# An attention and RWKV layer kernel: attention's loads one by one and a group ahead, groups in a new order, one bias load a head, and 8.0 instead of 1.5 between the inverse and its products

## The chip, the cores and the metric

The kernel runs on one core of one Trainium2 chip. The time is the device time of one launch in microseconds, the median of several runs. The core has five engines that the text names: TensorE (PE) for matmuls, VectorE (DVE), ScalarE (ACT), GpSimd (POOL), and SyncE (SP), which here only issues DMAs.

## The reference

Two trunk layers run over 128 context tokens and 512 latent tokens (a grid of 8 rows of 64), 1024 wide, in fp32. Each layer is

```python
proj = (x * (1 + scale1) + shift1) @ w_in
mix  = concat([o_rwkv, o_na, o_g], -1) @ w_out
x    = layer_norm(alpha * x + gate1 * mix)
gate, up = split((x * (1 + scale2) + shift2) @ w_ffn_in)
x    = layer_norm(alpha * x + gate2 * ((silu(gate) * up) @ w_ffn_out))
```

Three mixers read `proj`. RWKV (4 heads of 64) is a scan over the tokens in both directions:

```python
sk = einsum('bhvk,bhk->bhv', s, kk_t)
s  = s * w_t - sk * (a_t * kk_t) + v_t * k_t      # o_t = s @ r_t
```

Neighbourhood attention (na, 4 heads) lets a latent token see a window of 16 columns in all 8 rows, with a bias by relative position, and the context cache; columns outside are masked:

```python
s_nb = where(in_win, q @ kb * scale + rpb[:, dr, dc], NEG_INF)
p    = softmax(concat([s_nb, q @ k_ctx * scale]))
```

Grouped-query attention (gqa, 8 query heads on 2 key heads, RMS-normed and rotary) has each latent token see all latent tokens and 256 cached ones. Context tokens attend to context alone. Besides the two outputs the RWKV end states and the keys and values of the context are returned.

## The kernel before, in words

Everything stays transposed, features on partitions and tokens along the free axis. A product of fp32 weights is three matmuls on a high and a low part (`xh,whi`, `xl,whi`, `xh,wlo`), 320 tokens wide. Per layer the stages are the input projection (`proj_all`), `mixing` (attention), `mixed` (the output projection by w_out), and the tail with the feed-forward part.

**RWKV** is cut into chunks of 64 tokens, as 8 jobs per layer (two pairs of heads, two halves, two directions) in two slots of four jobs that run side by side. `rwkv_slot` takes each job through features, products, `inverse` and `states`. `inverse` (L757 to L800) inverts small triangular blocks on VectorE, copies the result into the tile `TB`, writes it and `XB` to DRAM by two DMAs from ScalarE's queue (`td<-TB` L793, `xd<-XB` L794) and reads them back in matrix form by four DMAs from GpSimd's queue (`T<-td` L797, `X<-xd` L799). Then it yields 1.5 (L800). `states` begins with a product that doesn't need them (`RV,N`); its second is `T,A` on PE, which needs `T`. From there on each product reads what the one before left: `N,X` and `X,N`, `T,A`, `X,N`, `AL,X`, `RV,ST` and `ST,RV`, `ST,A`, `S,A`, `RHO,S`; then the group norm of a finished half (`f,bmean`, `bmean,gnsq`, `ident,gnr`). I call this row of products the chain of a job.

**Attention** consists of units: six context pairs (`ctx_pair`), two na groups of four units (`na_pair`), four gqa groups of four units (`gqa_pair`), in this order. A unit makes scores of two heads (`ks,qs`), softmax on VectorE and ScalarE, transposes of the probabilities (`ident,prob`) and the products with the values (`pT,vw`, `pT,nvc`, `pT,gv`, `pT,gvc`); a group ends with `ident,sms`. The data come back from DRAM by SyncE's queue: queries `qs` (`stacked`, 256 KB, 4 buffers), keys `ks` (`doubled`, 2 x 384 KB, 3 buffers), the na values `vw` (`na_values`, 8 DMAs of 64 KB, 1 buffer) and the na bias (`na_bias`, 4 DMAs a head of 128x8x32 words, 2 buffers), to which GpSimd adds the column mask (L949). All loads of a group are written at once, where the group begins; those of the first group are written before the context pairs (`load_attn`).

**What sets the order.** Tasks are generators. `yield x` means: come back when the planner's clock `te.now` has gone on by x microseconds; this clock is the modelled time of the PE work that was emitted. `tick` steps all tasks that are due; `weave` steps the one that is due first, and sets the clock forward if none is. In `mixing` two attention tasks and RWKV's two slots run through `weave` until attention is at its end; `mixed` then begins the output projection and ticks through what RWKV has left. From the text thus written a scheduler sets each engine's order, and on the chip each engine runs its list in that order.

Of the kernel before, what the change touches and what calls it, by code (L numbers as in the profile page):

```python
# [8 lines left out]
F32 = mybir.dt.float32  # L9
F32R = mybir.dt.float32r  # L10
AF = mybir.ActivationFunctionType
ALU = mybir.AluOpType
# [4 lines left out]
P = 128  # L17
# [4 lines left out]
NLAT = 512  # L22
# [9 lines left out]
NA_LO = (0, 8, 24, 32)  # L32
NA_N = 32
# [50 lines left out]
class Build:  # L84
# [547 lines left out]
    def rwkv_job(self, l, ft, hb, d, slot, pool):  # L632
# [121 lines left out]
        def inverse():  # L754

            BT = J.BT
            bt = lambda name, n, tag=None: pool.tile([4 * NC] + n, F32, name=f"{name}{slot}", tag=f"{tag or name}{slot}", bufs=1)  # L757
            XB = bt("XB", [16, 16], "rt3")
            tmp = bt("tmpB", [512], "rt2")
            nc.gpsimd.memset(XB, 0.0)  # L760
            nc.gpsimd.memset(XB.rearrange("p i j -> p (i j)")[:, ::17], 1.0)

            def q8(t, i, j0, j1):

                b = t[:, 0, 0:1]
                return bass.AP(tensor=b.tensor, offset=b.offset + i * 16 + j0, ap=[list(b.ap[0]), [8 * 17, 2], [1, j1 - j0]])

            def q8m(t, i0, i1, j0, j1):

                b = t[:, 0, 0:1]  # L770
                return bass.AP(tensor=b.tensor, offset=b.offset + i0 * 16 + j0, ap=[list(b.ap[0]), [8 * 17, 2], [1, j1 - j0], [16, i1 - i0]])
            for i in range(6, -1, -1):
                m = 7 - i
                if m == 1:
                    nc.vector.tensor_copy(q8(XB, i, i + 1, 8), q8(BT, i, i + 1, 8))
                    continue
                t = tmp[:, :2 * m * m].rearrange("p (q k j) -> p q k j", q=2, k=m)
# [24 lines left out]
        def bmm(lhs, rhs, N, evac, swap=False):  # L802

# [117 lines left out]
    def load_attn(self, l):  # L921
        nc, I, at = self.nc, self.I, self.at
        self.nvc = at.tile([P, 2, 256], F32, name="nvc", bufs=1)
        nc.gpsimd.dma_start(self.nvc, I["c_na_v"][l])
        self.gvc = at.tile([P, 2, P], F32, name="gvc", bufs=1)
        self.units_ = self.units(l)
        first = next(self.units_)
        self.units_ = itertools.chain([first], self.units_)
        nc.gpsimd.dma_start(self.gvc, I["c_g_v"][l])

    def na_values(self, l, ft):

        nc = self.nc
        vw = self.at.tile([P, 4, 2, P], F32, name="vw", bufs=1)
        vr = self.vd.rearrange("(r c) f -> r c f", c=64)[:, :, ft * P:(ft + 1) * P]
        for j in range(4):
            for hf in range(2):
                nc.sync.dma_start(vw[:, j, hf, :], vr[hf * 4:hf * 4 + 4, NA_LO[j]:NA_LO[j] + NA_N, :])  # L938
        return vw

    def na_bias(self, l, hd):

        nc = self.nc
        bias = self.at.tile([P, 4, 8, NA_N], F32, name="bias", bufs=2)
        for j in range(4):
            b = self.rpx[0:1]
            off = hd * 15 * 16 * (RP - 1) + PAD + 15 + NA_LO[j] - 16 * j
            nc.sync.dma_start(bias[:, j], bass.AP(tensor=b.tensor, offset=b.offset + off, ap=[[RP - 1, P], [16 * (RP - 1), 8], [1, NA_N]]))  # L948
            nc.gpsimd.tensor_tensor(bias[:, j], bias[:, j], bc(self.nmask[:, j * NA_N:(j + 1) * NA_N], 1, 8), ALU.add)  # L949
        return bias  # L950

    def stacked(self, dram, h, name, n, bufs):

# [1 line left out]
        self.nc.sync.dma_start(self.r32(t), dram[:, h * CH:(h + 1) * CH, :])  # L955
        return t

    def doubled(self, dram, h):

        t = self.at.tile([P, 2, 768], F32R, name="ks", tag="ks", bufs=3)  # L960
        for u in range(2):
            self.nc.sync.dma_start(self.r32(t[u * CH:(u + 1) * CH]), dram[:, h * CH:(h + 1) * CH, :].rearrange("a p n -> p a n"))
        return t

    def out_parts(self, dram, hi, lo):
        self.nc.sync.dma_start(dram[0], self.r32(hi))
# [131 lines left out]
            yield from unit  # L1098

    def units(self, l):  # L1100
        def load(ft):
            bias = [self.na_bias(l, 2 * ft + h) for h in range(2)]
            vw, ks = self.na_values(l, ft), [self.doubled(self.nkd[ft], h) for h in range(2)]
            return vw, [(self.stacked(self.nqd[ft], h, "qs", NLAT, 4), ks[h], bias[h]) for h in range(2)]
        vw, qk = load(0)
        for kt in range(6):
            yield self.ctx_pair(l, kt)
        for ft in range(2):
            if ft:
                vw, qk = load(ft)  # L1110
            st = {}
            for j in range(4):
                yield self.na_pair(l, ft, j, qk, vw, st)
        for kv in range(2):
            ks = self.doubled(self.gkd, kv)
            for m in range(2):
                qs = [self.stacked(self.gqd[2 * m + u], kv, "qs", NLAT, 4) for u in range(2)]
                st = {}
                for t in range(4):
                    yield self.gqa_pair(l, kv, m, t, qs, ks, st)  # L1120

    def softmax(self, ps, n, negmax, scale, sums=None):

# [70 lines left out]
    def na_pair(self, l, ft, j, qk, vw, st):  # L1194
        nc = self.nc
# [4 lines left out]
        for h in range(2):  # L1200
# [10 lines left out]
            nc.vector.tensor_tensor_reduce(ps[:, 0:nw], ps[:, 0:nw], bias[:, j].rearrange("p r n -> p (r n)"), 1.0, mc, ALU.add, ALU.max, mx)  # L1211
# [400 lines left out]
```

## Time and profile before

| | |
|---|---|
| runs | 2167.08, 2173.63, 2172.19 us; median 2172.19 |
| the profiled execution | 2173.96 us, span 2172.2 us |
| PE busy | 2056.1 us (95%) |
| VectorE, ScalarE, GpSimd busy | 1304.0 us (60%), 909.6 us (42%), 250.5 us (12%) |
| chain that ended last | PE 78%, DMA 9%, DVE 5%, ACT 3%, issue 2% |
| DMA | 226.48 MB in 158276 packets, 88533 of them under 512 B |

The span of layer 0's attention is about 291 to 577 us, of layer 1's 1334 to 1635 us; the long stretches between and behind are the feed-forward parts and the projection. The busy line of the page's second part, 40 slices of 54 us, shows them: attention lies in slices 6 to 11 and 25 to 30, where PE's digits and those of the granted clock go down to 7 and 8. [...]

### The profile page before, as it was taken

What the parts mean: (1) busy time and instruction counts of PE and PEld (TensorE: products, weight loads), DVE (VectorE), ACT (ScalarE), POOL (GpSimd) and SP (SyncE); (2) the same over time, 40 slices, a digit from 0 to 9 for tenths busy, and PEclk for the clock granted to TensorE, in tenths of its full rate; (3) what the DMA queues carried; (4) which work ended last, traced back from release to release, by engine and by line L of the source; (5) the groups of instructions that cost most, each with busy time, mean ns of one, the idle gap of its engine ahead of it and who ended that gap; (6) DMA issues with size and microseconds to landing.
All of it is one profiled execution on the core that took longest, in us unless ns stands there. A gap on an engine that the chain in (4) does not pass through costs nothing.

```text
span 2172.2 us, 41222 instructions
## 1 busy us (share of the span) xinstructions
PE 2056.1 (95%) x16737; PEld 1863.3 (86%) x16737; DVE 1304.0 (60%) x2874; ACT 909.6 (42%) x1823; POOL 250.5 (12%) x435
## 2 busy tenths in 40 slices
PE   6989989799999999999999999879999999999997
PEld 4877877577889999999989887657779999999997
DVE  6536677586776666666766567657767533233247
ACT  3434455455563212222466445546555421221234
POOL 0012242121100000000020224311101000000000
PEclk9999998899999999999999999879999999999998
DMA  8555354110414444444431415521114122222223
GB/s 296 147 155 167 108 107 91 41 44 20 153 63 142 150 145 156 146 146 144 142 133 69 134 64 106 99 55 27 32 45 138 61 74 73 72 70 84 77 84 111
DMA packets 158276, 226.48 MB, mean 104 GB/s; under 512 B 88533, under 2 KB 99413, under 8 KB 157957
## 3 DMA queue, kind: packets, MB, share of 16 engines
q1 hardware_dynamic: 118244, 200.82, 29.7%
q0 software_dynamic: 7568, 17.83, 3.0%
q10 hardware_dynamic: 32274, 5.20, 1.4%
q8 instruction: 132, 2.16, 0.4%
q14 instruction: 58, 0.48, 0.1%
HBM read 198.37 MB, written 25.40 MB: 103 GB/s over the span
## 4 chain that ended last, share of the span: by engine, by line
PE 78%; DMA 9%; DVE 5%; ACT 3%; issue 2%; SPq 1%; POOL 0%; ACTq 0%; POOLq 0%; DVEq 0%
PE ps_s L72 44%; PE ps_rw L72 26%; PE ps_pv L72 5%; PE ps_rw L76 4%; DMA td<-TB 2%; DMA qs<-nqd 2%; DMA wmod<-in_w_mod 1%; DMA T<-td 1%; SPq L948 1%; ACT whi L277 0%; DVE wlo L278 0%; SPq L938 0%; DMA xa<-in_xT 0%; DMA c_raw<-in_cT 0%; DMA vw<-vd 0%
## 5 line engine op out<-in xcount | busy, mean ns | idle before, releaser
L72 PE MATMUL ps_s<-xh,whi 128*128 128x320 f32 x1312 | 420.7, 323 | 25.2 <-ACT xh L277 11.6
L72 PE MATMUL ps_s<-xh,wlo 128*128 128x320 f32 x1312 | 412.8, 315 | 2.5 <-DVE wlo L278 2.5
L72 PE MATMUL ps_s<-xl,whi 128*128 128x320 f32 x1312 | 412.6, 315 | 0.6 <-DVE xl L278 0.4
L72 PEld LDWEIGHTS ps_s<-xh,whi 128*128 128x128 f32 x1312 | 251.6, 192 | 48.7 <-ACT xh L277 13.7
L72 PEld LDWEIGHTS ps_s<-xh,wlo 128*128 128x128 f32 x1312 | 252.1, 192 | 7.1 <-DVE wlo L278 4.4
L72 PEld LDWEIGHTS ps_s<-xl,whi 128*128 128x128 f32 x1312 | 252.4, 192 | 5.8 <-issue 2.9
L278 DVE TENSOR_TENSOR wlo<-wraw,whi 128x1024 fp32r<-128x1024 f32 (+1 forms) x118 | 141.3, 1198 | 157.5 <-ACT whi L277 157.1
L72 PE MATMUL ps_s<-xh,flo 128*128 128x320 f32 x736 | 228.4, 310 | 0.0
L72 PE MATMUL ps_s<-xl,fhi 128*128 128x320 f32 x736 | 228.3, 310 | 0.0
L72 PE MATMUL ps_s<-xh,fhi 128*128 128x320 f32 x736 | 228.3, 310 | 0.0
L277 ACT CAST whi<-wraw 128x1024 fp32r<-128x1024 f32 (+1 forms) x118 | 121.2, 1028 | 246.4 <-PE ps_s L72 144.7
L277 ACT CAST fhi<-wraw 128x1024 fp32r<-128x1024 f32 (+1 forms) x82 | 83.3, 1016 | 206.1 <-PE ps_s L72 99.5
L72 PEld LDWEIGHTS ps_s<-xh,fhi 128*128 128x128 f32 x736 | 138.7, 188 | 0.1
L72 PEld LDWEIGHTS ps_s<-xl,fhi 128*128 128x128 f32 x736 | 138.7, 188 | 0.0
L72 PEld LDWEIGHTS ps_s<-xh,flo 128*128 128x128 f32 x736 | 138.6, 188 | 0.1
L278 DVE TENSOR_TENSOR flo<-wraw,fhi 128x1024 fp32r<-128x1024 f32 (+1 forms) x82 | 96.9, 1183 | 57.8 <-ACT fhi L277 57.8
L1431 ACT ACTIVATE sg<-ps_s 128x320 f32<-128x320 f32 x88 | 38.2, 434 | 189.5 <-PE ps_s L72 189.3
L1432 DVE TENSOR_TENSOR sg<-sg,ps_s 128x320 f32<-128x320 f32 x88 | 42.7, 485 | 123.1 <-ACT sg L1431 122.5
L72 PE MATMUL ps_s<-ks,qs 128*128 128x256 f32 (+1 forms) x384 | 101.9, 370 | 11.6 <-DMA qs<-nqd 6.8
L1278 DVE SCALAR_TENSOR_TENSOR z<-ps_rw,modT,z 128x128 f32<-128x128 f32 (+2 forms) x144 | 58.9, 435 | 89.7 <-PE ps_rw L72 89.5
L1287 POOL COPY lnS<-z 128x320 f32<-128x320 f32 x8 | 6.3, 786 | 917.1 <-DVE z L1278 892.6
L72 PE MATMUL ps_rw<-hh,flo 128*128 128x320 f32 x352 | 109.1, 310 | 0.6 <-DVE flo L278 0.6
(400 smaller groups left out, 4642.4 us busy)
## 6 DMA issues: line engine op xcount, KB each, us to landing
wraw<-in_w_ffn_in SPq DMA_DIRECT2D x88, 512.0 KB
wmod<-in_w_modT SPq DMA_DIRECT2D x66, 512.0 KB
wraw<-in_w_in_f SPq DMA_DIRECT2D x42, 512.0 KB
wraw<-in_w_ffn_out SPq DMA_DIRECT2D x48, 448.0 KB
wmod<-in_w_mod SPq DMA_DIRECT2D x48, 256.0 KB
wraw<-in_w_out SPq DMA_DIRECT2D x16, 512.0 KB
wraw<-in_w_ffn_out SPq DMA_DIRECT2D x16, 512.0 KB
ks<-nkd SPq DMA_DIRECT2D x16, 384.0 KB
```

The costliest lines, as they stand in the source:

```text
L72: self.eng.matmul(out, lhsT, rhs, **kw)
L76: self.eng.transpose(out, src, ident)
L277: self.nc.scalar.copy(hi, src)
L278: self.nc.vector.tensor_tensor(lo, src, self.r32(hi), ALU.subtract)
L948: nc.sync.dma_start(bias[:, j], bass.AP(tensor=b.tensor, offset=b.offset + off, ap=[[RP - 1, P], [16 * (RP - 1), 8], [1, NA_N]]))
L1278: nc.vector.scalar_tensor_tensor(z[:, a:b], ps[:, q], g, xa[:, q], ALU.mult, ALU.add)
L1287: nc.gpsimd.tensor_copy(self.lnS[c], z)
L1431: nc.scalar.activation(sg, pg, AF.Silu)
L1432: nc.vector.tensor_tensor(sg, sg, pu, ALU.mult)
```

## The change

There are four edits. `inverse` yields 8.0 instead of 1.5. The loads move out of the groups into a task of their own, `loads`, of rank 3, which issues them one at a time with a yield after each, a group ahead of its use; it holds the loads of a group back (`after`) until the units of an earlier group have begun and ended, and a unit whose loads aren't written yet forces them (`need`). The groups go na 0, gqa 0, gqa 1, na 1, gqa 2, gqa 3 instead of na 0, na 1, gqa 0 to 3. And the bias of a head comes as one DMA of 128x8x48 words into a raw tile `braw`, which shares its one buffer with `vw`; GpSimd adds the mask from there into eight small `bias` tiles. The count of masks stays 16 a layer, of bias DMAs it goes from 16 to 4.

```diff
@@ inverse
-            yield 1.5
+            yield 8.0
@@ load_attn
-        first = next(self.units_)
-        self.units_ = itertools.chain([first], self.units_)
-        nc.gpsimd.dma_start(self.gvc, I["c_g_v"][l])
+        self.loader = self.spawn(self.loads(l), 3)
@@ na_values
-        vw = self.at.tile([P, 4, 2, P], F32, name="vw", bufs=1)
+        vw = self.vw[ft] = self.at.tile([P, 4, 2, P], F32, name="vw", tag="vw", bufs=1)
...
+            yield 0.7
@@ na_bias
-        bias = self.at.tile([P, 4, 8, NA_N], F32, name="bias", bufs=2)
-        for j in range(4):
...
-            nc.sync.dma_start(bias[:, j], bass.AP(tensor=b.tensor, offset=b.offset + off, ap=[[RP - 1, P], [16 * (RP - 1), 8], [1, NA_N]]))
-            nc.gpsimd.tensor_tensor(bias[:, j], bias[:, j], bc(self.nmask[:, j * NA_N:(j + 1) * NA_N], 1, 8), ALU.add)
+        if hd % 2 == 0:
+            self.braw[hd // 2] = self.at.tile([P, 2, 8, 48], F32, name="braw", tag="vw", bufs=1)
+        raw = self.braw[hd // 2][:, hd % 2]
...
+        self.nc.sync.dma_start(raw, bass.AP(tensor=b.tensor, offset=b.offset + off, ap=[[RP - 1, P], [16 * (RP - 1), 8], [1, 48]]))
+
+    def na_masked(self, hd, j):
+        bias = self.bias[hd, j] = self.at.tile([P, 8, NA_N], F32, name="bias", bufs=8)
+        o = NA_LO[j] - 16 * j + 16
+        self.nc.gpsimd.tensor_tensor(bias, self.braw[hd // 2][:, hd % 2, :, o:o + NA_N], bc(self.nmask[:, j * NA_N:(j + 1) * NA_N], 1, 8), ALU.add)
+
+    def loads(self, l):
+        self.ks, self.qs, self.vw, self.braw, self.bias = {}, {}, {}, {}, {}
+        def after(*g):
+            while not self.hurry and any(self.left[i] for i in g):
+                yield 1.0
+        def na(ft):
+            for h in range(2):
+                self.na_bias(l, 2 * ft + h)
+                yield 1.0
+            for h in range(2):
+                self.qs[ft, h] = self.stacked(self.nqd[ft], h, "qs", NLAT, 4)
+                yield 1.3
+                yield from self.doubled(self.nkd[ft], h, (0, 2 * ft + h))
+            for j in range(4):
+                for h in range(2):
+                    self.na_masked(2 * ft + h, j)
+                yield 1.6
+            yield from self.na_values(l, ft)
+        def gqa(kv, m):
+            if m == 0:
+                yield from self.doubled(self.gkd, kv, (1, kv))
+            for u in range(2):
+                self.qs[2 + 2 * kv + m, u] = self.stacked(self.gqd[2 * m + u], kv, "qs", NLAT, 4)
+                yield 1.0
+        for n, (g, need) in enumerate(((0, ()), (2, ()), (3, (0,)), (1, (0, 2)), (4, (3,)), (5, (1,)))):
+            yield from after(*need)
+            yield from na(g) if g < 2 else gqa((g - 2) // 2, g % 2)
+            self.got.add(g)
...
+    def need(self, g):
+        self.hurry = True
+        while g not in self.got:
+            self.step(self.loader)
+        self.hurry = False
@@ units
+        def unit(g, j, st):
+            self.need(g)
...
+            self.left[g] -= 1
+        for g in (0, 2, 3, 1, 4, 5):
             st = {}
             for j in range(4):
-                yield self.na_pair(l, ft, j, qk, vw, st)
+                yield unit(g, j, st)
```

How the order moves is shown at three places; the numbers in names are serials of buffers and differ between the two kernels. The first is SyncE's list of loads where layer 0's attention begins. Before:

```order
L948 DMA bias<-rpx_1055 128x8x32 x8
L938 DMA vw<-vd_2436 128x1x128 x8
L962 DMA ks<-nkd_1128 64x2x768 x4
L955 DMA qs<-nqd_1127 128x1x512 x2
L962 DMA ks<-nkd_1128 64x2x768 x2
L955 DMA qs<-nqd_1127 128x1x512 x2
L962 DMA ks<-nkd_1128 64x2x768
L948 DMA bias<-rpx_1055 128x8x32 x8
L962 DMA ks<-nkd_1128 64x2x768
L962 DMA ks<-gkd_1571 64x2x768 x2
```

After:

```order
L949 DMA braw<-rpx_1055 128x8x48 x2
L998 DMA qs<-nqd_1127 128x1x512
L1005 DMA ks<-nkd_1128 64x2x768 x2
L998 DMA qs<-nqd_1127 128x1x512
L1005 DMA ks<-nkd_1128 64x2x768 x2
L938 DMA vw<-vd_2414 128x1x128 x8
L1005 DMA ks<-gkd_1571 64x2x768 x2
L998 DMA qs<-gqd_1570 128x1x512 x3
L1005 DMA ks<-nkd_1128 64x2x768 x2
L998 DMA qs<-gqd_1570 128x1x512
L1005 DMA ks<-nkd_1128 64x2x768
```

The bias has gone from eight rows ahead of everything to two, `qs` and `ks` of the first na group (`nqd`, `nkd`) stand ahead of `vw`, and the loads of the gqa groups (`gkd`, `gqd`) come between those of the two na groups.

The second is PE in layer 0's attention, from the other slot's last product (`RHO,S`) to the first `T,A` of the job that waited longest. Before:

```order
L72 MATMUL ps_rw<-RHO_3414,S_4223 64x64 x10
L72 MATMUL ps_pv<-pT,vw 64x128 x4
L72 MATMUL ps_pv<-pT,nvc 64x128 x4
L72 MATMUL ps_s_4447<-ks,qs 128x256
L72 MATMUL ps_s_4522<-ks,qs 128x512 x2
L72 MATMUL ps_s_4522<-ks,qs 128x256
L72 MATMUL ps_rw<-T_4275,A_3882 64x64
```

After, the last twelve rows up to the same `T,A`; twelve more rows lie between the other slot's `RHO,S` and the first of these:

```order
L72 MATMUL ps_s_4608<-ks,qs 128x512 x2
L72 MATMUL ps_s_4608<-ks,qs 128x256
L72 MATMUL ps_rw<-FT_4032,BK_4033 128x128 x3
L72 MATMUL ps_s_4608<-ks,qs 128x256
L72 MATMUL ps_s_4677<-ks,qs 128x512 x2
L72 MATMUL ps_rw<-f_561,w_1060 128x320
L72 MATMUL ps_rw<-f_575,a_1062 128x320
L72 MATMUL ps_pv<-pT,gv 64x128
L72 MATMUL ps_rw<-bmean,gnsq 128x2 x3
L76 MATMUL ps_rw<-ident,prob 128x128 x6
L72 MATMUL ps_s_4677<-ks,qs 128x256 x2
L72 MATMUL ps_rw<-T_4355,A_4028 64x64 x10
```

Between the two products there were five rows; there are 23 now, with scores, transposes and products of features (`FT,BK`) among them.

The third is PE at the end of layer 1's attention. Before, the last job's chain from `ST,A` on, with attention's transposes, value products and row sums between its steps:

```order
L72 MATMUL ps_rw<-ST_16919,A_17566 64x128 x10
L76 MATMUL ps_rw<-ident,prob 128x128 x6
L72 MATMUL ps_pv<-pT,gv 64x128
L72 MATMUL ps_rw<-S_17649,A_17567 64x64 x2
L72 MATMUL ps_pv<-pT,gv 64x128 x7
L72 MATMUL ps_pv<-pT,gvc 64x128 x4
L72 MATMUL ps_rw<-S_17649,A_17567 64x64 x4
L72 MATMUL ps_rw<-ident,sms 64x128 x3
L72 MATMUL ps_rw<-S_17649,A_17567 64x64 x2
L72 MATMUL ps_rw<-RHO_17102,S_17649 64x64 x10
L72 MATMUL ps_rw<-ident,sms 64x128 x5
L72 MATMUL ps_rw<-f_14403,bmean 128x320
```

After, the last job's chain from `T,A` on; ahead of it stand attention's last rows and 40 matmuls of the output projection:

```order
L72 MATMUL ps_rw<-T_17568,A_17369 64x64 x9
L72 MATMUL ps_rw<-N_17635,X_17567 64x64 x10
L72 MATMUL ps_rw<-X_17567,N_17635 64x64 x10
L72 MATMUL ps_rw<-T_17568,A_17370 64x64 x10
L72 MATMUL ps_rw<-X_17567,N_17672 64x64 x10
L72 MATMUL ps_rw<-AL_17373,X_17567 64x128 x10
...
L72 MATMUL ps_rw<-ST_17210,RV_17374 64x64 x9
L72 MATMUL ps_rw<-ST_17210,A_17697 64x128 x10
L72 MATMUL ps_rw<-S_17758,A_17698 64x64 x8
L72 MATMUL ps_rw<-RHO_17375,S_17758 64x64 x10
...
L72 MATMUL ps_rw<-xh_17531,whi 128x320
```

Nothing but the chain's own products stands between `T,A` and the norm any more; the output projection goes on behind it (24 matmuls from the last row on), and the attention has come to its end before. At the end of layer 0's attention the last chain stands likewise behind attention, there with 48 output matmuls between its steps.

## Rows read from the trace of the kernel before

**Rows 1.** TensorE's waits in layer 0's attention: us in total, times, longest.
```profile
PE ps_rw L72 <- DMA T<-td: 12.5, 4, 11.6
PE ps_s L72 <- DMA qs<-nqd: 3.9, 1, 3.9
```

**Rows 2.** TensorE's waits in layer 1's attention.
```profile
PE ps_rw L72 <- DMA T<-td: 15.6, 2, 8.5
PE ps_s L72 <- DMA qs<-nqd: 2.9, 1, 2.9
```

**Rows 3.** TensorE's records around layer 0's longest wait: start, us; idle in brackets.
```profile
404.24 0.44 PE L72 MATMUL ps_rw<-T,A 64*64 64x64 f32 x2 [11.60 <-DMA T<-td]
...
406.80 1.32 PE L72 MATMUL ps_rw<-T,A 64*64 64x64 f32 x18
...
416.30 0.80 PE L72 MATMUL ps_rw<-T,A 64*64 64x64 f32 x20
```

**Rows 4.** The chain of waits: start us, us, what.
```profile
308.07 15.54 DMA qs<-nqd
...
385.27 15.71 DMA td<-TB
401.50 2.60 DMA T<-td
...
1443.05 13.32 DMA td<-TB
```

**Rows 5.** SyncE's DMA issues where layer 0's attention begins.
```profile
290.21 8.32 SPq L948 DMA_DIRECT2D bias<-rpx  x8
298.57 4.81 SPq L938 DMA_DIRECT2D vw<-vd  x8
...
308.07 2.50 SPq L955 DMA_DIRECT2D qs<-nqd  x2
```

**Rows 6.** Windows, layer 0's attention: busy us (instructions) of each engine, PEclk, DMA share.
```profile
294.00:325.00 31.00, 24.91 (x307) 18.08 (x308) 23.64 (x80) 18.35 (x61) 13.88 (x19) 0.96 0.71 138
325.00:370.00 45.00, 42.97 (x429) 33.30 (x427) 31.49 (x106) 24.52 (x60) 13.15 (x20) 0.80 0.52 98
370.00:405.00 35.00, 20.65 (x238) 15.66 (x235) 18.73 (x66) 13.14 (x34) 4.06 (x8) 0.89 0.29 73
405.00:460.00 55.00, 53.97 (x589) 42.26 (x587) 40.34 (x107) 33.15 (x71) 10.07 (x16) 0.91 0.11 26
...
540.00:577.00 37.00, 35.20 (x447) 30.35 (x447) 26.11 (x64) 22.91 (x46) 2.22 (x5) 1.00 0.33 111
```

**Rows 7.** The same windows of layer 1's attention.
```profile
1337.00:1371.00 34.00, 28.39 (x332) 20.91 (x332) 23.88 (x78) 16.77 (x59) 14.02 (x21) 0.89 0.74 138
1371.00:1410.00 39.00, 34.98 (x320) 27.62 (x317) 27.20 (x96) 23.40 (x57) 11.66 (x16) 0.88 0.53 97
1410.00:1460.00 50.00, 34.07 (x390) 26.48 (x391) 29.48 (x93) 20.37 (x50) 9.20 (x18) 0.82 0.26 65
...
1590.00:1635.00 45.00, 41.30 (x459) 34.63 (x459) 29.36 (x70) 25.98 (x50) 3.18 (x6) 0.92 0.19 64
```

**Rows 8.** TensorE at the end of layer 1's attention, from its records.
```profile
1590.80 0.33 PE L72 MATMUL ps_rw<-T,A 64*64 64x64 f32 x2
...
1615.39 0.87 PE L72 MATMUL ps_rw<-ident,sms 128*64 128x128 f32 x10
...
1630.07 0.31 PE L72 MATMUL ps_s<-xl,whi 128*128 128x320 f32 x1
...
1634.76 0.31 PE L72 MATMUL ps_rw<-xh,fhi 128*128 128x320 f32 x1
```

**Rows 9.** Groups of TensorE in that stretch: busy us, mean ns, idle before.
```profile
L72 PE MATMUL ps_rw<-T,A 64*64 64x64 f32 x40 | 1.9, 224 | 0.0
...
L72 PE MATMUL ps_rw<-RV,ST 128*64 128x64 f32 x20 | 1.4, 236 | 0.6 <-DVE RV L837 0.5
...
L72 PE MATMUL ps_rw<-RHO,S 64*64 64x64 f32 x20 | 0.8, 218 | 0.0
```

More of the change, by code (lines that the diff above doesn't have):

```diff
@@ L925, in load_attn @@
         self.gvc = at.tile([P, 2, P], F32, name="gvc", bufs=1)
+        nc.gpsimd.dma_start(self.gvc, I["c_g_v"][l])
+        self.left, self.got, self.hurry = [4] * 6, set(), False
         self.units_ = self.units(l)
-        first = next(self.units_)
-        self.units_ = itertools.chain([first], self.units_)
-        nc.gpsimd.dma_start(self.gvc, I["c_g_v"][l])
+        self.loader = self.spawn(self.loads(l), 3)
     def na_values(self, l, ft):
         nc = self.nc
-        vw = self.at.tile([P, 4, 2, P], F32, name="vw", bufs=1)
+        vw = self.vw[ft] = self.at.tile([P, 4, 2, P], F32, name="vw", tag="vw", bufs=1)
         vr = self.vd.rearrange("(r c) f -> r c f", c=64)[:, :, ft * P:(ft + 1) * P]
@@ L938, in na_values @@
                 nc.sync.dma_start(vw[:, j, hf, :], vr[hf * 4:hf * 4 + 4, NA_LO[j]:NA_LO[j] + NA_N, :])
-        return vw
+            yield 0.7
     def na_bias(self, l, hd):
-        nc = self.nc
-        bias = self.at.tile([P, 4, 8, NA_N], F32, name="bias", bufs=2)
-        for j in range(4):
-            b = self.rpx[0:1]
-            off = hd * 15 * 16 * (RP - 1) + PAD + 15 + NA_LO[j] - 16 * j
-            nc.sync.dma_start(bias[:, j], bass.AP(tensor=b.tensor, offset=b.offset + off, ap=[[RP - 1, P], [16 * (RP - 1), 8], [1, NA_N]]))
-            nc.gpsimd.tensor_tensor(bias[:, j], bias[:, j], bc(self.nmask[:, j * NA_N:(j + 1) * NA_N], 1, 8), ALU.add)
@@ L950, in na_bias @@
-        return bias
+        if hd % 2 == 0:
+            self.braw[hd // 2] = self.at.tile([P, 2, 8, 48], F32, name="braw", tag="vw", bufs=1)
+        raw = self.braw[hd // 2][:, hd % 2]
+        b = self.rpx[0:1]
+        off = hd * 15 * 16 * (RP - 1) + PAD + 15 - 16
+        self.nc.sync.dma_start(raw, bass.AP(tensor=b.tensor, offset=b.offset + off, ap=[[RP - 1, P], [16 * (RP - 1), 8], [1, 48]]))
[3 more added lines that the diff above has]
+        self.nc.gpsimd.tensor_tensor(bias, self.braw[hd // 2][:, hd % 2, :, o:o + NA_N], bc(self.nmask[:, j * NA_N:(j + 1) * NA_N], 1, 8), ALU.add)
@@ L956, in stacked, with doubled @@
         return t
-    def doubled(self, dram, h):
-        t = self.at.tile([P, 2, 768], F32R, name="ks", tag="ks", bufs=3)
+    def doubled(self, dram, h, key):
+        t = self.ks[key] = self.at.tile([P, 2, 768], F32R, name="ks", tag="ks", bufs=3)
         for u in range(2):
             self.nc.sync.dma_start(self.r32(t[u * CH:(u + 1) * CH]), dram[:, h * CH:(h + 1) * CH, :].rearrange("a p n -> p a n"))
-        return t
+            yield 2.0
     def out_parts(self, dram, hi, lo):
@@ L1100, in units @@
     def units(self, l):
[L1101 to L1105, printed above, removed]
         for kt in range(6):
             yield self.ctx_pair(l, kt)
-        for ft in range(2):
-            if ft:
-                vw, qk = load(ft)
+        def unit(g, j, st):
+            self.need(g)
+            if g < 2:
+                qk = [(self.qs[g, h], self.ks[0, 2 * g + h], self.bias[2 * g + h, j]) for h in range(2)]
+                yield from self.na_pair(l, g, j, qk, self.vw[g], st)
+            else:
+                kv, m = divmod(g - 2, 2)
+                yield from self.gqa_pair(l, kv, m, j, [self.qs[g, u] for u in range(2)], self.ks[1, kv], st)
+            self.left[g] -= 1
+        for g in (0, 2, 3, 1, 4, 5):
             st = {}
             for j in range(4):
-                yield self.na_pair(l, ft, j, qk, vw, st)
[L1114 to L1120, printed above, removed]
+                yield unit(g, j, st)
     def softmax(self, ps, n, negmax, scale, sums=None):
@@ L1210, in na_pair @@
             mx = self.tp.tile([P, 1], F32, name="mx", tag="mx", bufs=4)
-            nc.vector.tensor_tensor_reduce(ps[:, 0:nw], ps[:, 0:nw], bias[:, j].rearrange("p r n -> p (r n)"), 1.0, mc, ALU.add, ALU.max, mx)
+            nc.vector.tensor_tensor_reduce(ps[:, 0:nw], ps[:, 0:nw], bias.rearrange("p r n -> p (r n)"), 1.0, mc, ALU.add, ALU.max, mx)
             nm = self.tp.tile([P, 1], F32, name="nm", tag="nm", bufs=4)
```

## The prediction

> **What bounds the kernel now.** I read first what TensorE (PE) waits for, stage by stage, then the chain of waits, then the windows with the granted clock, then PE's own records at the places where the change moves something. In the two attention stretches PE's longest waits have one cause: the second product of an RWKV job (`T,A`) waits for the read-back `T<-td`, 12.5 us in layer 0 and 15.6 us in layer 1, nearly all of it in three waits, of 11.6, 8.5 and, by subtraction, 7.1 us [rows 1, 2]. The next cause is the first attention load, `qs<-nqd`, with 3.9 and 2.9 us [rows 1, 2]. The chain shows why `T` is late: the write `td<-TB` is issued at 385.27 and takes 15.71 us, the read after it 2.60 us, and at 1443.05 the write takes 13.32 us [rows 4]. From the write at 385.27 to `T,A` at 404.24 are 19.0 us, of which PE stood for 11.60 [rows 3, 4]: it found 7.4 us of other work and then had to stand, because `T,A` was next in its order.
>
> A third loss is not a wait. Behind the 11.6 us wait the 18 small matmuls of `T,A` take 1.32 us, twelve microseconds later 20 of the same take 0.80 us [rows 3]: 73 ns each against 40 ns, the lower clock level against the upper. A mean granted clock c in a window means that (1 - c) of PE's busy time there was lost to the lower level. For layer 0 that gives 0.04 x 24.91 + 0.20 x 42.97 + 0.11 x 20.65 + 0.09 x 53.97 = 16.8 us [rows 6], for layer 1 0.11 x 28.39 + 0.12 x 34.98 + 0.18 x 34.07 = 13.4 us and in its last stretch 0.08 x 41.30 = 3.3 us [rows 7]. The feed-forward stages have none of these waits, and the change doesn't touch them.
>
> **The delay of 8.0 (term A).** It removes nothing and adds no instruction. Each job's states are emitted 6.5 us of planner time later, so that much more attention work stands between the write of `TB` and `T,A` in PE's order. The order printed above shows it for the longest wait: five rows stood between the other slot's `RHO,S` and `T,A`, now 23. If a planner microsecond is worth a real one, the three waits shrink to 5.1, 2.0 and 0.6 us and 20 of the 28.1 us go. The order shows rather more than that at each of the three, so I leave 4 us and book **24**, with 18 and 28 as ends. What is late next at these places is the attention itself: its scores wait for softmax on VectorE and ScalarE, which in these windows have a quarter of their time or more left [rows 6].
>
> **Loads one by one, bias in one load a head, new group order (term B).** SyncE issues eight bias loads in 8.32 us and eight `vw` loads in 4.81 us before the first `qs`, whose load then takes 15.54 us [rows 4, 5]. Now two bias loads stand first, at the same 1.04 us an issue 2.1 us, and `vw` goes behind `qs` and `ks`. The first `qs` is thus issued some 10 us sooner, more than the 3.9 and 2.9 us that PE waits for it. The new pieces are 192 bytes long instead of 128 and a quarter as many; as no row prices such a piece, the bounds are eight old loads' cost (nothing gained) and a quarter of it. What is late next is VectorE, busy for 23.64 of the 31 us [rows 6], so I book **5** of 6.8 us, with 0 and 7 as ends. Two waits are new. The eight POOL masks of a group stand in one piece and wait for the bias load; in layer 0 one job's two `T` reads stand behind them on POOL, and `T,A` behind these. And the first `vw` load shares its buffer with the raw bias, so on SyncE it waits for the masks, with the `ks` and `qs` of the next group queued behind it; PE needs those only after four units of the first group. Both lie beside other work, at nothing. If that cover fails, POOL holds the read by what it is busy in that window, 13.88 us [rows 6] less its old share, which I bound at 6 us, once.
>
> **The clock (term C).** If waits go, so should the low stretches behind them. I don't take all. In the window 325 to 370 PE is busy for 42.97 of 45 us and yet the clock is 0.80 [rows 6]: the `qs` load lands at 323.61 [rows 4], just ahead of it, and then no long wait follows, only thin work (small matmuls, with VectorE busy for 31.49 us beside them). Of the 30.2 us ahead of the tail (16.8 and 13.4) I take two thirds, **20**, with 7 and 30 as ends. [...]
>
> **The end of each attention (term D, a price).** The delay adds up: four jobs a slot, 6.5 each, 26 us of planner time. So RWKV now ends behind attention. Before, layer 1's last `T,A` begins at 1590.80 with attention beside it to 1616.26, and the next stage's first matmul at 1634.76, 18.5 us behind attention [rows 8]. After, by the order, 40 output matmuls follow attention, then the whole last chain with nothing beside it, then 24 matmuls. The matmuls step by 0.147 us (32 from 1630.07 to 1634.76 [rows 8]): 5.9 and 3.5 us. The chain's own PE time is nine groups, from 1.9 us for `T,A` to 0.8 for `RHO,S`, together 11.2 us [rows 9], and some 2 us for the norm. Its 12 steps each wait for an eviction of the one before; 0.5 us of this shows even with other work in between [rows 9], so I take 0.6 to 1.2 us a step, 11 in all. That is 24 us alone, and 33 from attention's end to the next stage instead of 18.5, 15 more; but attention ends 11 us sooner because the chain's work is no longer in it, which leaves 4. Alone and thin, the chain may also run at the lower level, up to 13 us more, of which 3.3 are paid already [rows 7]; I add 4. So layer 1 pays 8 (2 to 20). In layer 0 48 output matmuls (7 us) lie between the chain's steps, and the stretch now has 1.8 us of idle in 37 [rows 6]: 11 less 7 is 4, rounded up to 5 (0 to 12). Together **-13**, with -2 and -32 as ends.
>
> **The projection stage (term E).** About one chain's work (11.2 us) moves from the projection into the attention. Where PE is full that is neutral; where not, a gap opens or closes: 0, within 6 either way.
>
> **Sum.** 24 + 5 + 20 - 13 = 36 us off the profiled execution's 2173.96 us, 2138; that execution lies 1.8 us above the median of the runs, so **2136 us**.
>
> **The rivals.** (1) Everything returns and the tail stays hidden: 28 + 7 + 30 - 2 = 63, 2109 us. For it: the slow stretches begin at the waits [rows 3]. Against: the order at the end of layer 1. (2) The waits go but the clock stays low because the stretch is thin: 24 + 5 + 7 - 13 = 23, 2149 us. For it is the window 325 to 370. (3) The change doesn't do what it says: the planner's clock jumps on when no task is ready, the delay finds no work to put in between, and only the loads pay, 5 us: 2167 us. Against it stand the 23 rows. (4) Slower: a slot's own length becomes what ends each layer. Then each layer's end moves by the full 26 us, 52 in all, in place of term D, against A and B of 29 and a clock that gives 9 at most since chains run alone: 14 us more, 2186 us. It decides from the point where a slot's eight stages take longer than the PE work beside them; the tail of layer 1 has reached it, the rest by the order not.
>
> **How the numbers follow.** Forecast 0.50, (1) 0.18, (2) 0.12, (3) 0.08, (4) 0.12. A measurement of this kernel can tell about 0.3% (6.5 us) from no change. Faster by more holds the forecast, (1) and (2), 0.80; (3) lies within it, 0.08; (4) is slower, 0.12. The range leaves out (4), the half of (3) above it and the lowest part of (1), 0.04 each: **2104 to 2166**.
>
> **What would show it.** Right: `T<-td` under 8 us in PE's waits, `qs<-nqd` under 3; a granted clock above 0.95 in the first 110 us of each attention; in layer 1 some 10 us of PE idle between attention's end and the next stage, released by VectorE and ScalarE. Wrong: a new wait for `braw`, `vw` or `bias` on PE or VectorE (term B), a clock still at 0.8 to 0.9 with the waits gone (term C), or a tail longer by 20 us a layer (term D).

## The result, and the profile after

The change makes the kernel slower: 2194.7 us median (2189.7 to 2199.6) against 2172.5, a ratio of 1.0107 with a 95% interval of 1.0079 to 1.0136. The profiled execution took 2194.37 us with a span of 2192.2. I had forecast 2136 and a range that ended at 2166. Of all executions behind this document one, of the changed kernel with `BT` free, took 3228 us at a granted clock of 0.55; without it that kernel's median is 2164.3 us instead of the 2165.2 given below. The granted clock is the share of full speed that the profile gives for TensorE. Taken in windows of 1 us, it is 1.00 in 2013 of the 2172 of the execution before, 0.50 in 126 and between the two in 33; these two are the upper and the lower level of the prediction. At [rows 3] it is 0.50 from 404.2 to 414 us and 1.00 from 416.3 to 417.1.

TensorE's waits in layer 0's attention, the view of [rows 1], now read:

```profile
PE ps_rw L72 <- DVE tmpB L778: 5.7, 1, 5.7
PE ps_rw L72 <- DMA T<-td: 5.5, 1, 5.5
PE ps_rw L72 <- DVE nm L1252: 2.9, 1, 2.9
```

and in layer 1's, the view of [rows 2]:

```profile
PE ps_rw L72 <- DVE S L893: 7.6, 4, 6.0
PE ps_rw L76 <- DVE pT L1194: 7.0, 1, 7.0
PE ps_s L72 <- ACT prob L1169: 4.4, 2, 4.0
PE ps_rw L72 <- DVE gnr L613: 3.4, 2, 2.7
PE ps_rw L72 <- DMA T<-td: 2.5, 3, 1.6
```

The wait for `T` went as forecast, from 28.1 to 8.0 us, and `qs` no longer stands in the list; the first scores of layer 0 begin 22.5 us after the start of the attention instead of 31.7. In their place stand waits for VectorE: under `tmpB`, a step of the inverse, and under `nm`, a step of attention's softmax, each time with `AL,X` next on TensorE, whose `X` VectorE wrote just before; for `S` of the chain; and for `pT`, the eviction of attention's transposes (the copy out of the tile that TensorE wrote). One of 4.0 us is for ScalarE's `prob`. The windows that answer to [rows 6] (us, busy per engine, clock, DMA) are

```profile
286.00:316.00 30.00, 28.69 (x244) 20.09 (x243) 20.14 (x73) 17.59 (x60) 14.75 (x20) 0.89 0.59 129
316.00:365.00 49.00, 40.76 (x452) 31.48 (x446) 32.50 (x106) 26.20 (x65) 5.80 (x10) 0.93 0.35 80
365.00:420.00 55.00, 49.57 (x540) 39.09 (x540) 36.90 (x98) 29.06 (x63) 15.75 (x26) 0.91 0.18 45
...
547.00:580.00 33.00, 30.15 (x310) 24.65 (x307) 17.17 (x43) 11.12 (x23) 1.68 (x3) 0.90 0.32 107
```

and those of layer 1, which answer to [rows 7]:

```profile
1327.00:1360.00 33.00, 27.24 (x302) 20.08 (x301) 24.52 (x88) 20.49 (x66) 12.78 (x21) 0.79 0.58 124
1360.00:1400.00 40.00, 38.30 (x443) 29.43 (x440) 26.31 (x86) 22.99 (x58) 8.37 (x11) 1.00 0.40 94
1400.00:1440.00 40.00, 29.06 (x250) 22.16 (x248) 23.91 (x60) 20.43 (x40) 11.09 (x17) 0.89 0.19 45
...
1602.00:1649.00 47.00, 34.78 (x357) 30.25 (x354) 22.91 (x54) 14.26 (x32) 7.72 (x9) 0.78 0.15 40
```

I had wanted a clock above 0.95 in the first 110 us of each attention. It is 0.89 to 0.93 in layer 0, and 0.79, 1.00 and 0.89 in layer 1, where TensorE stood idle for 11 of the 40 us from 1400 on. The end of layer 1, which answers to [rows 8], from TensorE's records:

```profile
1601.55 1.09 PE L72 MATMUL ps_rw<-ident,sms 128*64 128x128 f32 x16
...
1618.26 0.29 PE L72 MATMUL ps_rw<-T,A 64*64 64x64 f32 x2 [1.63 <-DMA T<-td]
...
1633.38 0.75 PE L72 MATMUL ps_rw<-RHO,S 64*64 64x64 f32 x20
...
1649.16 0.31 PE L72 MATMUL ps_rw<-xh,fhi 128*128 128x320 f32 x1
```

Attention's last row sums end at 1602.64, the last job's `T,A` begins at 1618.26, 16 us behind them, the next stage at 1649.16. Counted from the start of the last row-sum matmul, this tail is 46.8 us long, where it was 18.8. In layer 0 the tail went from 17.0 to 33.1 us. Of the signs that I had named for a right forecast one came here: TensorE is idle for 12 of the 47 us from 1602 on.

Before, the last chain ended with attention in both layers: its last `RHO,S` matmul starts 1.9 us behind attention's last row-sum matmul in layer 0 and 0.7 us ahead of it in layer 1. After, it starts 20.9 and 31.5 us behind it, 51 us later in all. The rows of before, layer 0's and layer 1's:

```profile
559.71 0.43 PE L72 MATMUL ps_rw<-ident,sms 128*64 128x128 f32 x2
...
561.19 0.78 PE L72 MATMUL ps_rw<-RHO,S 64*64 64x64 f32 x20
...
1614.71 0.75 PE L72 MATMUL ps_rw<-RHO,S 64*64 64x64 f32 x20
1615.39 0.87 PE L72 MATMUL ps_rw<-ident,sms 128*64 128x128 f32 x10
```

To see where the 20 us of the two profiled executions lie, I cut every stretch into windows of some 10 us and added up, for each, the time in which TensorE was idle and (1 - clock) x busy, an estimate of what a granted clock below 1.00 cost. Both attentions together, and both tails (idle, clock loss, and the length of each tail):

| kernel | attention: idle | clock | tails: idle | clock | length |
|---|---|---|---|---|---|
| before | 53.8 | 27.8 | 3.7 | 2.7 | 17.0, 18.8 |
| after | 48.0 | 34.8 | 15.0 | 10.7 | 33.1, 46.8 |
| new order alone | 73.9 | 42.1 | 4.1 | 1.2 | 18.3, 17.0 |
| delay alone | 52.0 | 34.7 | 18.9 | 15.7 | 48.2, 49.1 |
| before, `T` and `X` free | 33.3 | 28.0 | 4.1 | 2.7 | 17.1, 19.3 |
| before, `BT` free | 29.1 | 14.9 | 3.9 | 2.8 | 17.1, 19.2 |
| delay alone, `BT` free | 36.9 | 26.6 | 14.6 | 9.9 | 44.3, 44.4 |
| before, 4.0 ahead of the inverse | 37.1 | 34.5 | 2.2 | 0.0 | 17.0, 26.0 |

From before to after: -5.8 and +7.0 in attention, +11.3 and +8.0 in the tails, 0.1 elsewhere: 20.6 of the 20.0 us. Attention lost 20 us of waits for `T` and got 14 of others back. (The other kernels of the table are the experiments' below; one execution each, not always one near its kernel's median.)

### The profile page after: what moved, and what is told of

The parts are those of the page before. It is cut to its first block, busy times and chain, and to the rows that moved or that the text cites. A ratio compares the mean times of both kernels' runs of the same rounds, so it can differ in the third digit from the quotient of the medians.

```text
span 2192.2 us, 41196 instructions
## 1 busy us (share of the span) xinstructions
PE 2069.1 (94%) x16737; PEld 1874.9 (86%) x16737; DVE 1298.9 (59%) x2874; ACT 904.1 (41%) x1819; POOL 247.8 (11%) x435
## 2 busy tenths in 40 slices
DMA packets 133315, 223.85 MB, mean 102 GB/s; under 512 B 63573, under 2 KB 74453, under 8 KB 132997
## 4 chain that ended last, share of the span: by engine, by line
PE 80%; DVE 7%; DMA 6%; ACT 3%; issue 2%; POOL 1%; SPq 0%; DVEq 0%; ACTq 0%; POOLq 0%
PE ps_s L72 44%; PE ps_rw L72 28%; PE ps_pv L72 5%; PE ps_rw L76 3%; DMA BT<-md 1%; DMA wmod<-in_w_mod 1%; DMA td<-TB 1%; DMA md<-X 1%; ACT whi L277 1%; DMA xd<-XB 1%; DVE tmpB L778 0%; DMA T<-td 0%; DMA c_raw<-in_cT 0%; DMA wraw<-in_w_out 0%; DVE tmpB L787 0%
## 5 line engine op out<-in xcount | busy, mean ns | idle before, releaser
L72 PE MATMUL ps_rw<-hh,wlo 128*128 128x320 f32 x352 | 108.8, 309 | 0.1
```

The costliest lines, as they stand in the source:

```text
L72: self.eng.matmul(out, lhsT, rhs, **kw)
```

## The experiments

Each was timed against the kernel before on the same chip; medians, with the ratio's interval. An edit is made in the changed kernel where its comment names no other. Theory A at first was that the delay costs, theory B that loads and order do.

### Which part costs

```diff
# loads only
-            yield 8.0
+            yield 1.5
# delay only, in the kernel before
-            yield 1.5
+            yield 8.0
# last job short
-            yield 8.0
+            yield 8.0 if self.jobs[slot] else 1.5
# delay 4
-            yield 8.0
+            yield 4.0
```

> The changed kernel with the yield behind the inverse set back to 1.5, so that only the loads, the bias and the new group order are left of the change. Theory A (the delay costs: it pushes RWKV's last chain behind attention, and what it saves in T waits is lost again): 2160 to 2175 us, the time from the last row-sum product of attention to the next stage near that of the kernel before (17 and 19 us), T<-td waits back near 20 to 28 us. Theory B (loads and group order cost, by new waits on VectorE): 2185 to 2200 us, and VectorE's waits for BT<-md stay above 12 us in layer 1.

> The kernel before with 8.0 in place of 1.5 behind the inverse and nothing else. Theory A: 2185 to 2200 us, tails of 30 us or more behind attention in both layers, T<-td waits under 10 us. Theory B: faster than before, 2140 to 2160 us, since the T waits go and no other wait comes.

> The changed kernel with 1.5 instead of 8.0 for the last job of each slot alone; the first three jobs of a slot keep 8.0. If the tail is what costs (theory A), its chain begins some 6 us sooner in each layer, and the time falls by 8 to 15 us to 2180 to 2187; theory B: within 4 us of the changed kernel's 2195, as the tail lies elsewhere.

> The changed kernel with 4.0 in place of 8.0: 2.5 us of planner time a job more than before instead of 6.5. Theory A: the price goes with the delay, so about two thirds of the way back, 2172 to 2182 us, with tails of some 22 and 30 us. Theory B: 2185 to 2197 us whatever the delay.

Measured: loads only 2181.8 (1.0031 to 1.0064), delay only 2209.9 (1.0162 to 1.0209), last job short 2198.6 (1.0114 to 1.0160), delay 4.0 2172.0 (0.9984 to 1.0028). Neither theory holds alone. The delay by itself costs 39 us, more than theory A had, the rest by itself 11, and the two together 22. Delay 4.0 came out as theory A had it, with tails of 19.8 and 33.6 us. Shortening the last job mended layer 0's tail (33.1 to 22.2 us) but not layer 1's (47.3); both attentions became some 5 us longer, and it won nothing, against theory A.

### Where the time goes in layer 1

At a place of layer 1's attention in the changed kernel, VectorE's records are:

```profile
1440.83 0.16 DVE L775 COPY XB<-BT 40x2 f32<-40x2 f32 x1 [9.41 <-DMA BT<-md]
...
1443.00 0.41 DVE L1194 COPY pT<-ps_rw 128x256 f32<-128x256 f32 x1
```

and TensorE's

```profile
1443.46 1.54 PE L76 MATMUL ps_rw<-ident,prob 128*128 128x128 f32 x6 [7.04 <-DVE pT L1194]
```

VectorE stands for 9.41 us at the first step of an inverse (`XB<-BT`), since the read `BT<-md` isn't there: `BT` is the first round trip through DRAM of a job, `md` written by ScalarE's queue and read back by GpSimd's, as `T` is the second. The eviction `pT` of attention stands behind it in VectorE's list, and TensorE waits 7.04 us for that. Three more of TensorE's waits in the two attentions end in the same way, 1.5 to 3.6 us behind a stand of VectorE for `BT`. VectorE's records there, then TensorE's:

```profile
332.52 0.16 DVE L775 COPY XB<-BT 40x2 f32<-40x2 f32 x1 [6.06 <-DMA BT<-md]
...
436.60 0.16 DVE L775 COPY XB<-BT 40x2 f32<-40x2 f32 x1 [4.21 <-DMA BT<-md]
...
1403.04 0.59 DVE L775 COPY XB<-BT 40x2 f32<-40x2 f32 x1 [4.79 <-DMA BT<-md]
```

```profile
334.06 2.40 PE L72 MATMUL ps_rw<-AL,X 64*64 64x128 f32 x20 [5.67 <-DVE tmpB L778]
...
438.77 1.96 PE L72 MATMUL ps_rw<-AL,X 64*64 64x128 f32 x14 [2.89 <-DVE nm L1252]
...
1406.63 0.48 PE L72 MATMUL ps_rw<-S,A 64*64 64x64 f32 x4 [5.97 <-DVE S L893]
```

The four waits make 21.6 us. VectorE's waits for `BT` are, before, after, and with the new order alone (below):

```profile
DVE XB L775 <- DMA BT<-md: 12.5, 4, 6.7
```

```profile
DVE XB L775 <- DMA BT<-md: 26.9, 6, 9.4
```

```profile
DVE XB L775 <- DMA BT<-md: 19.3, 4, 6.7
```

This made theory V: VectorE standing for `BT`, with attention behind it, takes the gain. Against it stood theory S: the slots' own length in planner time, which leaves the last chain alone behind attention.

```diff
# slot 20 (e8: also yield 4.0 for 8.0)
-            self.spawn(self.rwkv_slot(l, slot, bp)).ready += 40.0 * slot
+            self.spawn(self.rwkv_slot(l, slot, bp)).ready += 20.0 * slot
# order only (in the kernel before; each group still loads where it begins)
-        for ft in range(2):
...
+        for g in (0, 2, 3, 1, 4, 5):
# BT yield, at the head of inverse
+            yield 5.0
             BT = J.BT
```

> The changed kernel with its second slot started 20 instead of 40 us of planner time behind the first. Theory S (the length of a slot's four jobs ends each layer; the delay made the slots longer): the last chain begins up to 20 us sooner in each layer, the tails behind attention fall from 33 and 47 to some 20 and 28 us, the time to 2165 to 2182. Theory V (VectorE, standing at the first step of an inverse for BT<-md, holds up attention, wherever the slots lie): within 8 us of 2195, with the BT wait of VectorE still above 20 us.

> The kernel before with the new group order (na 0, gqa 0, gqa 1, na 1, gqa 2, gqa 3) alone: loads at the head of each group, four bias loads a head, yield 1.5. If the order is what makes the loads-only kernel slower than before (2181.8): 2177 to 2186. If the loads task or the bias load does: 2166 to 2175.

> The changed kernel with a yield of 5.0 ahead of the inverse, so that its first VectorE step is emitted later than the read BT<-md. Theory V: VectorE's wait for BT falls from 26.9 to under 8 us, TensorE's waits for VectorE's evictions go, and the time falls by 10 to 20 us, to 2175 to 2185. Theory S: the slots are 20 us longer once more, the time rises to 2205 to 2225, although the BT wait goes.

> The changed kernel with 4.0 in place of 8.0 and the second slot 20 us sooner. Theory S: the T waits stay near 10 us and the tails fall below those of the kernel before (17 and 19 us), 2150 to 2165 us, faster than both. Theory V: near 2172, as with 4.0 alone.

Measured: slot 20 2181.4 (1.0025 to 1.0063), with tails of 20.9 and 27.1 us, as S had it, though VectorE's wait for `BT` stayed at 27.2 us; order only 2198.6 (1.0084 to 1.0166), above both forecasts; `BT` yield 2199.9 (1.0101 to 1.0178), between the two; delay 4.0 with slot 20 2210.6 (1.0151 to 1.0215), against both theories: its tails are 18.8 and 18.7 us, near those of before, but the attentions are 22 and 7 us longer. That the slots' round trips fall on each other there is likely and not shown; VectorE's wait for `BT` is the largest of all kernels:

```profile
DVE XB L775 <- DMA BT<-md: 42.7, 11, 10.9
```

The yield ahead of the inverse didn't take the wait for `BT` away (27.9 us), so it says nothing on V; but it lengthened each slot by 20 us of planner time and the tails went from 33.1 and 46.8 to 55.0 and 68.4 us, 22 each, which is S. A longer tail isn't its own price, though: for 43 us of tails the time rose by 5 (15 between the profiled executions), as the two attentions became 29 us shorter. The new order costs 27 us alone. Its chain of waits at one place of layer 0 reads

```profile
by line: DMA md<-X 57.8%; DMA BT<-md 40.0%; issue 5.2%; PE ps_rw L76 3.4%; PE ps_pv L72 2.9%; DVE tmpB L778 2.4%; DVE RHO L863 1.9%; DVE XB L775 1.2%; DVE XB L779 1.2%; POOLq L723 0.3%
...
324.53 5.59 DMA BT<-md
...
330.14 0.17 DVE XB L775
...
330.89 0.27 DVE RHO L863
...
331.21 0.48 PE ps_rw L76
```

two legs of 8.10 and 5.59 us for `BT`, then the inverse's steps, then the eviction `RHO`, and only then TensorE.

### Loads without the new order, and `T` out of the way

```diff
# loads, old order (with 1.5, and with 4.0 behind the inverse)
-        for n, (g, need) in enumerate(((0, ()), (2, ()), (3, (0,)), (1, (0, 2)), (4, (3,)), (5, (1,)))):
+        for n, (g, need) in enumerate(((0, ()), (1, (0,)), (2, (0,)), (3, (1,)), (4, (2,)), (5, (3,)))):
-        for g in (0, 2, 3, 1, 4, 5):
+        for g in range(6):
# T free (in the kernel before); X alike from self.xd[8]
-                nc.gpsimd.dma_start(J.T[hs[h]], self.mat(tdr, h))
+                nc.gpsimd.dma_start(J.T[hs[h]], self.mat(self.td[8], h))
# BT free (in the kernel named)
-            nc.gpsimd.dma_start(J.BT, self.blocks(md))
+            nc.gpsimd.dma_start(J.BT, self.blocks(self.td[8]))
```

> The changed kernel's loads task and bias loads with the old order of groups (na 0, na 1, gqa 0 to 3) and the old yield of 1.5. Theory O (the new order costs some 27 us, as the order alone did, and the loads give some 17 of them back): 2150 to 2160 us, faster than before. Theory I (the loads gain only because the new order made them late: in the old order there is little to give back): 2166 to 2176 us.

> The same with 4.0 behind the inverse. With the new order 4.0 was 10 us better than 1.5. If that gain is the T waits and doesn't hang on the order: 8 to 12 us less than with 1.5 and the old order. If it is luck of how the two slots fall against the attention units: anything within 20 us to either side of it.

> The kernel before, but T and X are read from a scratch of zeros that no job writes, so the round trip through DRAM is left out (the writes are still made, the reads still issued and waited for). It prices terms A and C of the prediction together. By the prediction's numbers (24 and 20 us, nothing for the tail): 2125 to 2135 us. If the waits only change their name, as in the changed kernel: 2155 to 2172.

> The changed kernel, but BT is read from a scratch of zeros that no job writes, so the inverse's first VectorE step doesn't wait for the products' round trip through DRAM (the write is still made, the read still issued). Theory V (VectorE standing there is what took the gain): 2165 to 2178 us, TensorE's waits for VectorE's evictions in attention under 5 us. Theory S (the slots' length): the slots get shorter by the round trip too, but only where it was waited for; 2180 to 2192 us with tails still above 25 us in layer 1.

Measured: loads in the old order 2182.7 (1.0029 to 1.0070) and with 4.0 2186.1 (1.0044 to 1.0085), so both theories on the first miss: the loads cost 12 us in the old order too; and the gain of 4.0 does hang on the order, here it costs 3 us. In the kernels called free a read goes to a scratch of zeros that no job writes, so the round trip is left out, while the writes and the read itself are still made. `T` and `X` free: 2154.6 (0.9881 to 0.9935), at the lower edge of the forecast by which the waits only change their name. This is the price of what I had booked at 44 us: 16 by the medians, 14 to 26 by the interval. With `T` there at once, TensorE meets the other wait. VectorE and then TensorE in that kernel:

```profile
331.78 0.16 DVE L775 COPY XB<-BT 40x2 f32<-40x2 f32 x1 [7.16 <-DMA BT<-md]
```

```profile
332.85 0.47 PE L76 MATMUL ps_rw<-ident,prob 128*128 128x128 f32 x1 [5.21 <-DVE RHO L863]
```

`BT` free in the changed kernel: 2165.2 us (0.9941 to 0.9998), 30 less than the changed kernel, as theory V had it.

### Both theories at once

> The control for the three below: the kernel before with BT read from a scratch of zeros that no job writes, so no inverse waits for the products' round trip (the writes are still made). Its VectorE stands 12.5 us for BT. Theory V (what VectorE stands there is lost): 2155 to 2165 us. If other work hides it: 2165 to 2175.

> The new group order alone (2198.6 us, 27 above before) with BT free. Theory V (the new order brings attention's evictions on VectorE behind inverses that stand for BT): the 27 us shrink to under 10 against the control. If the order costs by something else (the gqa loads that come late at the head of their group, or the clock): the distance to the control stays above 18 us.

> The delay of 8.0 alone (2209.9 us, 39 above before) with BT free. Theory S (the slots end too late, tails of 48 and 49 us): against the control 25 to 40 us remain, with tails above 35 us. Theory V: under 15 us remain.

> The changed kernel with BT free once more, for its profile: near 2165 us as measured. Theory V alone: the attention stretches lose under 15 us each to TensorE's idle time and the tails stay at 33 and 47 us. With S beside it: the tails fall too, since the slots no longer wait for BT, to 25 and 35 us.

> Loads, bias and new order without the delay (2181.8 us, 11 above before) with BT read from a scratch of zeros that no job writes; it closes the table of the parts with BT free. If the loads' price without the delay is that of the BT wait alone, as the order's was: at or below the control's 2130.6. If the 20 us that the loads gave back beside the delay (2186 to 2166) are there without it: 2108 to 2115. If the loads themselves cost: above 2136.

| parts | as it is | `BT` free |
|---|---|---|
| before | 2172 | 2130.6 (0.9798 to 0.9830) |
| new order | 2198.6 | 2131.5 (0.9798 to 0.9831) |
| loads, bias, new order | 2181.8 | 2128.8 (0.9764 to 0.9818) |
| delay | 2209.9 | 2186.0 (1.0039 to 1.0089) |
| all of the change | 2194.7 | 2166.7 (0.9946 to 0.9988) |

The control, the kernel before with `BT` free, fell by 42 us, far more than theory V had asked, and with `BT` free the order and the loads cost nothing (1 us more and 2 less, within what the runs can tell); what they cost otherwise hangs on the round trips. The delay costs 55 us there instead of 39, more than theory S had. The 16 between is the size of what `T` free had shown, which fits a delay that saves some 16 us of waits for `T` and pays 55; that the two add up in this way isn't shown. Freeing `BT` is more than taking a wait away: the inverse no longer hangs on its job's products, the scheduler puts it earlier (its first step on VectorE begins 35 to 67 us sooner in layer 0), and `T` is there long before its product; the waits for `T` were gone altogether in the kernel before with `BT` free, with the old 1.5. So the 42 us are the price of both round trips in the row, not of VectorE's 12.5 us of standing alone. The scheduler also moved other instructions (about one in ten of TensorE's matmuls stands in another place in its list), so a part of the 42 may be that. That zeros in the operands raised the clock is unlikely: with `T` and `X` zero its loss in attention stayed at 28.0 us.

With the delay and `BT` free, the windows of the two tails show what is left:

```profile
556.00:600.00 44.00, 38.46 (x372) 27.92 (x373) 20.33 (x51) 12.60 (x28) 2.07 (x4) 0.88 0.20 59
```

```profile
1604.00:1648.00 44.00, 35.11 (x377) 29.77 (x378) 20.28 (x52) 13.96 (x29) 1.88 (x4) 0.82 0.11 33
```

44 us each, with TensorE at 0.88 and 0.82 of its clock and idle for 5.5 and 8.9 us. All of the change with `BT` free has tails of 32.0 and 39.5 us, and 15.4 and 13.8 us of idle in its attentions: V's attention with most of S's tail. Here a tail is near its price: these two are together 35 us longer than the control's, and the kernel is 36 us slower; with the delay alone they are 52 us longer, and it is 55 slower. Between the profiled executions of the latter and the control the attention of layer 0 is also 21 us longer and that of layer 1 13 shorter.

### A better version

```diff
# the kernel before, at the head of inverse
+            yield 4.0
             BT = J.BT
```

> The kernel before with a yield of 4.0 ahead of the inverse: VectorE's step that reads BT is emitted later, and each slot is 16 us longer by the planner. If the BT wait can be covered this way: VectorE's wait for BT falls from 12.5 to under 5 us and the time to 2140 to 2160. If the slots' length is what counts (both ends of attention lie within 19 us of the last chain already): 2175 to 2200, with tails of 30 us or more.

Measured: 2164.3 us (0.9935 to 0.9981), 4 us above what I had expected if it worked, below what theory S had, and faster than both kernels, by 9 us (0.4%) than the one before. Its waits:

```profile
PE ps_rw L72 <- DVE S L894: 5.2, 10, 1.2
...
PE ps_rw L72 <- DMA T<-td: 2.7, 1, 2.7
```

```profile
DVE XB L776 <- DMA BT<-md: 22.1, 8, 5.1
```

A delay ahead of the first round trip covers a part of both: `T` falls from 28.1 to 2.7 us, while VectorE, against what I had expected, stands for `BT` longer in all, eight times, but never for longer than 5.1 us. So the sum of these waits doesn't order the kernels: this one has 22.1 us of them and the kernel before 12.5. The tail of layer 1 grows from 18.8 to 26.0 us only. That it gains more than the same 4.0 behind the inverse is measured with the old loads here and the new ones there, so the two aren't compared cleanly.

## Why the prediction was wrong

**What bounds the kernel.** I read TensorE's list of waits and took the cause of the longest as the bound. VectorE's list, which I didn't read, had the wait for `BT`, 12.5 us; without the round trip that it ends, the waits for `T` vanish with no delay at all. `T` was late in a row of two. (A slip that nothing hangs on: the clock loss of layer 0 adds up to 16.7 us, not 16.8.)

**Term A** got its waits (28.1 to 8.0 us; I had said 4 would stay) and not its time. Attention's idle fell by 5.8 us, not 24. "What is late next at these places is the attention itself" was the step that failed: next late was VectorE behind `BT`, in four of the five waits of over 2 us that TensorE had in the two attentions for other engines; one, of 4.0 us, was for softmax.

**Term C** was the largest miss. The clock's loss in attention went from 27.8 to 34.8 us instead of falling by 20. With every wait for `T` out of the way it stayed at 28.0; it fell, to 14.9, only with `BT` free, which took both waits away. In the changed kernel TensorE waited for VectorE instead and was slow behind these waits just the same. Ahead of the 7.04 us wait for `pT` the granted clock is 1.00 (1433 to 1436.4 us); behind it, it is 0.50, and six transposes take 1.54 us, which elsewhere take 0.82 to 0.88 at 1.00. Behind the 5.67 us wait it is 0.50 too, and 20 `AL,X` take 2.40 us, which take 1.31 at 1.00.

**Term B.** The wait for `qs` went. It brought nothing that can be measured (2128.8 with loads, bias and order against 2130.6, both with `BT` free). That the new order could cost had no term at all; alone it costs 27 us, through the round trips.

**Term D** was seen at the right place and priced by the wrong sum. The chain itself was right: in layer 1 it takes 20 us from `T,A` to the first `ident,gnr`, where I had 24 with the norm. But `T,A` came 16 us behind attention, where I had 5.9 us of matmuls: the other slot's group norm stood ahead of them, with 3.0 us of waits, the first twelve of the matmuls ran at a granted clock of 0.50 (1609.0 to 1612.1 us), most of them 0.27 us apart, the later ones at 1.00 and 0.147 apart, and 1.6 us of waiting for `T` came last. Behind the chain came 10 us, where I had 3.5. For a slow chain I had added 4 us out of up to 13, an estimate that takes its 13 us once more, as at 0.50; by (1 - clock) x busy the loss in layer 1's tail went from 2.7 to 7.6. So there were 46.8 us where I had 33, and in layer 0 the tail became 33.1 where it was 17.0. And I set the tail against an attention that ends 11 us sooner in each layer, as if TensorE were full there; the attentions became only some 7 and 5 us shorter, with all that terms A to C brought. With `BT` free the delay alone costs 55 us, where I had 13.

**Rival (4)** had the mechanism and the size: each layer's end moves by the slot's 26 us, 52 in all, 2186 us. The last chain came out 51 us later against attention's end (19 and 32), and the tails grew by 44. The 38 us that it set against them came to some 30, in attentions and stretches ahead of them that became shorter as work moved, not in waits and clock, so that its sum came near is in part luck. I gave it 0.12, because I read from the order that only layer 1's tail had reached the point. Layer 0's had reached it too: before, the last chain ended within 2 us of attention in both layers. That each microsecond added to a slot comes out behind isn't so: the 4.0 ahead of the inverse, 16 us a slot, moved the last chain by 17 us in layer 1 and not at all in layer 0. **Term E**, booked at nothing, can't be measured by itself: the stretches ahead of the two attentions became 5.5 and some 11 us shorter.

Still open: why the loads take 20 us off the delay's price with `BT` free (2186.0 to 2166.7) and 17 off the new order's (2198.6 to 2181.8), but cost 12 in the old order, which wasn't run with `BT` free; and why 20 us between the slots helps with 8.0 and hurts with 4.0. The two slots, the round trips and attention's units shift against each other in each of these kernels, and these shifts are as large as the 22 us that the change costs.

## What to carry to other kernels

Before you move work behind a wait, read the waits of every engine that stands in order with it; the engine that is waited for may itself wait for the link before. Where two rows of work end together, a delay in either moves the end: ask for the slack at the end of each row first, and count the delay as often as it is paid. A longer tail has to be set against what the stretch ahead of it loses. And measure what a wait is worth by taking its cause away; the 28 us of waits that I led with were worth some 16, slow clock and all.

## What the runs showed of the hardware that I had not expected

With the new loads the bias comes in a quarter as many pieces, of 192 bytes instead of 128. The DMA packets went from 158276 to 133315, and TensorE's wait for `qs` went too; no run tells the smaller count from the place of `qs` ahead of `vw`. With `BT` free the time didn't move by it (2131.5 us with the new order alone, 2128.8 with the loads). And the granted clock was 0.50 behind waits for VectorE as behind a wait for a DMA: 20 `AL,X` took 2.40 us at 0.50 behind the 5.67 us wait for VectorE and 1.31 later, at 1.00; behind the 11.60 us wait for a DMA of [rows 3] it was 0.50 for some 10 us. In the kernel with the new order alone, where TensorE stood idle in attention for 73.9 us, the clock cost another 42.1 us.
